# Loads of v on SyncE's queue instead of GpSimd's in the opening of a WKV recurrence kernel

## The chip, the cores and the metric

The kernel runs on one core of one Trainium2 chip. The metric is the device time of one execution in microseconds (us). A core has five engines with instruction streams of their own: TensorE (PE in the profile; PEld are its weight loads), VectorE (DVE), ScalarE (ACT), GpSimd (POOL) and SyncE (SP). Data moves between device memory and the core's SBUF by DMA, over 16 DMA engines that all queues of the core share. In this kernel two queues carry nearly everything: q0, whose transfers GpSimd issues in software, and q1, whose transfers SyncE issues.

## The reference

For each of 16 batches and each of 256 channels a recurrence runs over 2048 time steps, with a running maximum `pp` that keeps the exponentials in range:

```python
for t in range(seq_len):
    ww = u + kk
    qq = np.maximum(pp, ww)
    e1 = np.exp(pp - qq)
    e2 = np.exp(ww - qq)
    output[b, t, :] = (e1 * aa + e2 * vv) / (e1 * bb + e2 + 1e-08)
    ww = pp - w + kk
    qq = np.maximum(ww, kk)
    e1 = np.exp(ww - qq)
    e2 = np.exp(kk - qq)
    aa = e1 * aa + e2 * vv
    bb = e1 * bb + e2
    pp = qq
```

`k` and `v` are float32 of shape (16, 2048, 256), 33.55 MB each, and so is the output.

## The kernel before

The time steps are cut into 16 chunks of 128 steps, and each chunk into two halves of 64. A "pair" n is a tile of k and a tile of v with 128 time steps on the partitions, 4 batches and 256 channels: 512 KB each. There are 64 pairs; pair n belongs to chunk n // 4 and to the batches 4 * (n % 4) and the three after it. Below, kn and vn are the two tiles of pair n, counted from 0, so the fourth pair is n = 3.

For each pair these steps run; the short name in brackets is the one that the planner at the end of the kernel uses.

- Load k (`LK`, `load_k`) and v (`LV`, `load_v`).
- Bring k into the rounded 32-bit form that TensorE's fast float product reads, in a buffer of the pool `kr` (4 buffers). How this is done is chosen by `how(n)`: "D" rounds on VectorE and "P" on GpSimd (`RK`, `round_k`, line 200), both from a plain load into another buffer (`kf`, 5 buffers; for the first three pairs, a free output buffer `ot`). "C" loads with a conversion in the DMA, straight into `kr`, and needs no rounding. The string `FIRST` gives the choice for the first pairs, `PLAN` = "DDDP" repeats for the rest.
- Two products on TensorE, `rows` (`R`, line 207) and `logs` (`L`, line 213), form the logarithms of the weights in one of two PSUM tiles X, once with the matrix NLE (q = 0) and once with NLZ (q = 1). ScalarE takes the exponential of each (`X`, line 216).
- Cast v to bfloat16 (`CV`, `cast_v`, line 220): on VectorE for n < 10 (`EARLY`), on GpSimd from then on. Multiply it onto the weights on VectorE (`TV`, line 225), and sum each half chunk on TensorE (`S`, line 252).
- When a chunk's four pairs are summed, the state runs on: copy of the sums (`CS`, line 258), turn (`TU`, line 265), logarithm (`SL`, line 269), a scan and offsets on VectorE (lines 274 to 282), weights (`SW`, line 288), a scan (`CH`), a spread (`SS`) and the turn back (`TK`, line 309; `BK`, line 313).
- About ten pairs later the output follows: denominator and numerator on TensorE (`DEN`, `NUM`, line 329), logarithm and exponential of the denominator on ScalarE (lines 341 and 346), a product on VectorE (`MUL`, line 361) and three stores on SyncE (`ST`, lines 374 and 367). The first store is issued at 44.18 us.

Every step has a place, a number on one axis for all engines. The planner takes, again and again, the step with the lowest place whose predecessors are done and whose buffers are free, and writes its instructions into the streams of its engines; `keep_in_program_order` holds that order. On the chip each engine goes through its own stream in order and waits at an instruction until the semaphores that it needs are there. An issue of a load is such an instruction: if its buffer isn't free yet, all that is behind it on its engine waits too. The planner knows the buffers by the counts in `free`: 4 `kr` (K), 5 `kf` (KP), 4 `vr` for v (V), 8 `ot` (OT), 2 `vb` (VB). A `kr` buffer is free again after the second product `logs` of its pair; a `vr` buffer after the cast of its v.

In the opening, SyncE issues k0, k1, v0, k2, v1 and v2 (`BYSP` = 3) into output buffers. GpSimd then issues k3, k4, v3, k5, v4, k6, v5, k7, v6, k8, v7, k9, v8, k10, v9, k11, v10, k12, v11, k13, v12 in this order (lines 117, 121 and 114), rounds k11, casts v10, and goes on with loads and casts. k3 to k10 are "C". Matmuls on zeros into the tile TURN (line 155) are filled in between.

Of the kernel before, what the change touches and what calls it, by code (L numbers as in the profile page):

```python
# [15 lines left out]
def kernel(  # L16
# [9 lines left out]
    K = tc.keep_in_program_order  # L26
    PE, DVE, SC, POOL, SP = nc.tensor, nc.vector, nc.scalar, nc.gpsimd, nc.sync
# [11 lines left out]
    UNTIL = 16  # L39
    SHARE = 0.2  # L40
    BYSP = 3
    EARLY = 10
    PLAN = "DDDP"
    NK, NKP, NV, NVB, NRD, NOT = 4, 5, 4, 2, 2, 8
    RS = 2.0 ** -20
    CAP = 54.0
    BIG = 1e30
    FIRST = "DDDCCCCCCCC"
    VOT = 3
    XT = 8  # L50
    BYPOOL = 52
# [47 lines left out]
    def rows_of(x, n):  # L99
        c, p = divmod(n, 4)  # L100
        return x[4 * p:4 * p + 4, c * TC:(c + 1) * TC, :].rearrange("n t d -> t n d")
# [3 lines left out]
    def how(n):  # L105
        return "D" if n < BYSP else FIRST[n] if n < len(FIRST) else PLAN[n % len(PLAN)]

    def raw(pool, tag):
        return pool.tile([128, 4, Dm], F32, tag=tag, name=tag)

    def load_k(n):
        if how(n) != "C":
            KR[n] = raw(opool, "ot") if n < BYSP else raw(kppool, "kf")
            K((SP if n < BYSP else POOL).dma_start(out=KR[n], in_=rows_of(k, n)))  # L114
        else:
# [2 lines left out]

    def load_v(n):
        vr = raw(opool, "ot") if n < VOT else raw(vpool, "vr")  # L120
        K((SP if n < BYSP else POOL).dma_start(out=vr, in_=rows_of(v, n)))  # L121
        VR[n] = vr

    WUf = rpool.tile([128, 2, D], F32, tag="rd", name="WUf")[:, 0, 0:Dm]
# [93 lines left out]
    def cast_v(n):  # L218
        vb = vbpool.tile([128, 4, Dm], BF16, tag="vb", name="vb")
        K((DVE if n < EARLY else POOL).tensor_copy(vb, VR.pop(n)))  # L220
        VB[n] = vb
# [166 lines left out]
    for n in range(NP):  # L388
        c, j = divmod(n, 4)
        early = n < BYSP  # L390
        vb = "OT" if n < VOT else "V"
# [9 lines left out]
        else:  # L401
            free["OT"] -= 1
        step(("LV", n), n + P["LV"], load_v, (n,), [("LV", n - 1)] + ([("LK", n)] if n else []), vb)
        if how(n) != "C":
            step(("RK", n), put("RK"), round_k, (n,), [("LK", n), ("RK", n - 1)], "K", [kb])
# [91 lines left out]
```

## Time and profile before

| what | value | where it is from |
|---|---|---|
| median of 3 runs | 288.26 us (288.19 to 288.63) | times |
| profiled execution | 288.83 us, of which the span is 287.1 us | times, page |
| granted TensorE clock | 0.99 | page |
| PE, DVE, ACT, POOL busy | 268.5, 248.5, 259.0, 175.7 us | page, part 1 |
| moved by DMA | 101.20 MB, 352 GB/s mean | page, part 2 |
| q0 (GpSimd) | 65.42 MB in 21200 packets | page, part 3 |
| q1 (SyncE) | 35.14 MB in 37280 packets | page, part 3 |
| ACT busy, 17.2 to 44.6 us | 19.30 of 27.40 us | windows |
| ACT busy, 44.6 to 258 us | 209.50 of 213.40 us | windows |
| issue to landing of k3, k4, v3 | 8.9, 9.5, 10.3 us (issued 5.18, 6.08, 6.81) | DMA view, one window for each |
| issue to landing of k5, v4, k6, v5 | 6.6, 8.3, 8.8, 9.5 us (issued 12.00, 13.15, 14.21, 14.94) | DMA view, one window for each |
| q0's first tile data | after 9.8 us (until then 32 packets with less than 0.005 MB) | DMA view, 2 to 9.8 us |
| GpSimd before line 117 until PE has freed a buffer | 8.4 us in 6 waits, longest 4.3 | waits |
| GpSimd before line 121 until VectorE has cast a v | 7.0 us in 4 waits, longest 2.9 | waits |

The span is the time from the first to the last instruction on the core; the profiled execution's own time is 1.73 us longer. Landing is the moment at which the transfer's semaphore says that all of its bytes are there. In the timeline a row gives the start and the duration, the engine, the line, the operation, the output and input tiles and, in square brackets, how long the engine was idle just before and who ended that. The chain of waits is followed back from the last instruction to what released each step.

### The profile page before, as it was taken

The numbers are of one execution on the slowest core, as the hardware profiler recorded it, in microseconds if no ns is written. First come the engines' busy times: TensorE is split into PE (matmuls) and PEld (weight loads), VectorE is DVE, ScalarE is ACT, GpSimd is POOL, SyncE is SP. The second block draws the span as 40 slices with busy tenths as digits, with TensorE's granted clock in tenths as the row PEclk, the third lists the DMA queues.
The fourth block names the chain that finished last, engine by engine and source line by source line (L and its number), as shares of the span: only waits on it lengthen the run. The fifth ranks groups of instructions, "written<-read, shape, count | busy, mean of one in ns | idle before, by whom it ended". The sixth has DMA issues, their size and how long they took to land.

```text
span 287.1 us, 7961 instructions
## 1 busy us (share of the span) xinstructions
PE 268.5 (94%) x3215; PEld 134.8 (47%) x3215; DVE 248.5 (87%) x422; ACT 259.0 (90%) x291; POOL 175.7 (61%) x219
## 2 busy tenths in 40 slices
PE   6997999999999999999899999999999999997860
PEld 6443544454545455454445445454544454453530
DVE  5678799899898989897998989999898989889860
ACT  1786679999999999999999999999999999998990
POOL 8365476875757676874757686675766685421320
PEclk9999999999999999999999999999999999999996
DMA  6999999999999999999999999999999999955896
GB/s 220 349 351 346 349 350 352 393 382 390 381 392 389 391 392 389 389 353 388 391 393 387 381 391 388 390 376 394 383 391 369 393 391 382 369 160 142 217 275 191
DMA packets 58669, 101.20 MB, mean 352 GB/s; under 512 B 5152, under 2 KB 43688, under 8 KB 58632
## 3 DMA queue, kind: packets, MB, share of 16 engines
q0 software_dynamic: 21200, 65.42, 64.8%
q1 hardware_dynamic: 37280, 35.14, 36.5%
q8 instruction: 25, 0.41, 0.6%
q10 hardware_dynamic: 152, 0.14, 0.2%
q14 instruction: 12, 0.10, 0.1%
HBM read 67.12 MB, written 33.55 MB: 351 GB/s over the span
## 4 chain that ended last, share of the span: by engine, by line
PE 53%; DMA 23%; ACT 10%; DVE 8%; issue 3%; SPq 0%; POOL 0%; DVEq 0%; ACTq 0%; POOLq 0%
DMA out_dram<-ot 19%; PE X L213 14%; PE X L329 10%; PE num L329 8%; PE X L207 8%; PE TURN L155 7%; PE TOT L252 4%; ACT rd L341 4%; ACT EZR L216 3%; DVE ot L361 3%; DMA kr<-in_k_dram 3%; ACT rd L346 2%; DMA WUf<-in_u_dram 2%; DVE EZR L225 2%; PE TOT L265 1%
## 5 line engine op out<-in xcount | busy, mean ns | idle before, releaser
L216 ACT ACTIVATE EZR<-X 128x1024 bf16<-128x1024 f32 x128 | 126.8, 1014 | 11.5 <-PE X L213 11.5
L220 POOL CAST vb<-vr 128x1024 bf16<-128x1024 f32 x54 | 56.4, 1044 | 69.2 <-DVE EZR L225 67.8
L225 DVE TENSOR_TENSOR EZR<-EZR,vb 128x2048 bf16<-128x2048 bf16 x64 | 77.8, 1217 | 0.4
L361 DVE TENSOR_TENSOR ot<-num,rd 128x1024 f32<-128x1024 f32 x60 | 73.2, 1219 | 4.3 <-ACT rd L346 3.9
L346 ACT ACTIVATE rd<-rd 128x1024 f32<-128x1024 f32 (+1 forms) x65 | 68.0, 1046 | 2.0
L341 ACT ACTIVATE rd<-X 128x1024 f32<-128x1024 f32 (+1 forms) x65 | 65.8, 1012 | 2.9 <-PE X L329 1.1
L155 PE MATMUL TURN<-Z 128*128 128x192 bf16 x271 | 53.0, 262 | 1.5 <-DVE Z L139 1.4
L207 PE MATMUL X<-WU,CO 64*64 64x512 bf16 x512 | 51.9, 390 | 1.7 <-DVE WU L182 1.0
L121 POOL DMA_DIRECT2D vr<-in_v_dram x61 | 46.4, 761 | 7.0 <-DVE vb L220 7.0
L155 PEld LDWEIGHTS <-Z 128*128 128x128 bf16 x271 | 24.5, 101 | 50.6 <-issue 49.1
L213 PE MATMUL X<-kr,NLE 128*128 128x512 f32 x128 | 45.6, 437 | 0.7 <-DMA kr<-in_k_dram 0.7
L213 PE MATMUL X<-kr,NLZ 128*128 128x512 f32 x128 | 45.5, 436 | 0.0
L114 POOL DMA_DIRECT2D kf<-in_k_dram x53 | 40.2, 758 | 0.0
L200 DVE CAST kr<-kf 128x1024 fp32r<-128x1024 f32 x39 | 32.0, 849 | 4.2 <-DMA kf<-in_k_dram 4.0
L207 PEld LDWEIGHTS <-CO 64*64 64x64 bf16 x512 | 15.8, 104 | 32.2 <-issue 27.2
L329 PE MATMUL X<-EZR,S 64*64 64x512 bf16 x256 | 26.2, 394 | 1.7 <-ACT rd L341 1.0
L329 PE MATMUL num<-EZR,SN 64*64 64x512 bf16 x240 | 24.2, 386 | 2.2 <-DVE ot L361 2.2
L329 PE MATMUL X<-cb,Id 64*64 64x512 bf16 x256 | 25.8, 376 | 0.0
L329 PE MATMUL X<-EZR,Id 64*64 64x512 bf16 x256 | 25.8, 376 | 0.0
L252 PE MATMUL TOT<-EZR,OH 128*32 128x256 bf16 x512 | 23.7, 277 | 0.8 <-DVE EZR L225 0.5
L329 PE MATMUL num<-cb,IdN 64*64 64x512 bf16 x240 | 23.9, 376 | 0.0
L329 PE MATMUL num<-EZR,IdN 64*64 64x512 bf16 x240 | 23.9, 376 | 0.0
(69 smaller groups left out, 270.5 us busy)
## 6 DMA issues: line engine op xcount, KB each, us to landing
vr<-in_v_dram POOLq DMA_DIRECT2D x61, 512.0 KB, 7.9
kf<-in_k_dram POOLq DMA_DIRECT2D x53, 512.0 KB, 8.7
out_dram<-ot SPq DMA_DIRECT2D x64, 256.0 KB, 10.0
out_dram<-ot SPq DMA_DIRECT2D x116, 128.0 KB, 9.8
kr<-in_k_dram POOLq DMA_DIRECT2D x8, 512.0 KB, 9.5
ot<-in_k_dram SPq DMA_DIRECT2D x3, 512.0 KB, 5.2
ot<-in_v_dram SPq DMA_DIRECT2D x3, 512.0 KB, 8.4
out_dram<-ot POOLq DMA_DIRECT2D x11, 128.0 KB, 4.0
```

The lines of the kernel that those rows point to most:

```text
L114: K((SP if n < BYSP else POOL).dma_start(out=KR[n], in_=rows_of(k, n)))
L121: K((SP if n < BYSP else POOL).dma_start(out=vr, in_=rows_of(v, n)))
L155: K(PE.matmul(TURN[:, 0:192], Z[:, 0:128], Z, start=first, stop=True, skip_group_check=True))
L207: K(PE.matmul(X[a][o:o + HS, i, :].rearrange("p (n d) -> p n d", n=2), CO[r:r + HS, q, :], WU[r:r + HS, :].unsqueeze(1).broadcast_to([HS, ...
L213: K(PE.matmul(X[a][:, i, :], (NLE, NLZ)[q], km[:, i, :], start=False, stop=True, skip_group_check=True))
L216: K(SC.activation(ez(n)[:, q, 1], X[a], ACT.Exp))
L220: K((DVE if n < EARLY else POOL).tensor_copy(vb, VR.pop(n)))
L225: K(DVE.tensor_mul(ez(n)[:, :, 0], ez(n)[:, :, 1], vb.unsqueeze(1).broadcast_to([128, 2, 2, D])))
L329: K(PE.matmul(out_tile[o:o + HS, i, :], left, right, start=s == 0, stop=s == 2, tile_position=(r, o), skip_group_check=True))
L341: K(SC.activation(RD[n][:, i], X[a][:, i], ACT.Ln, scale=RS))
L346: K(SC.activation(RD[n][:, i], RD[n][:, i], ACT.Exp, scale=-1.0))
L361: K(DVE.tensor_mul(o.rearrange("p (i n) d -> p i (n d)", i=2)[:, i], NUM[n][:, i], RD[n][:, i]))
```

## The change

SyncE issues the loads of v for n = 3 to 13 too (`BYV` = 14; the destination buffers are the same as before), and k11 is loaded with its conversion ("C" as the twelfth letter of `FIRST`) instead of plain and then rounded on GpSimd. The step `RK 11` is gone, and k11 takes a `kr` buffer at its load. Nothing else is edited.

```diff
     BYSP = 3
+    BYV = 14
     EARLY = 10
...
-    FIRST = "DDDCCCCCCCC"
+    FIRST = "DDDCCCCCCCCC"
...
     def load_v(n):
         vr = raw(opool, "ot") if n < VOT else raw(vpool, "vr")
-        K((SP if n < BYSP else POOL).dma_start(out=vr, in_=rows_of(v, n)))
+        K((SP if n < BYV else POOL).dma_start(out=vr, in_=rows_of(v, n)))
```

In the changed program GpSimd's stream has k3 to k11, k12, k13, the cast of v10, k14, k15, the cast of v11, v14, k16, v15 and so on. SyncE's stream has its six loads as before, then v3 to v13, then the first store. The streams of TensorE, VectorE and ScalarE hold the same instructions in the same order as before.

## The prediction

> **What bounds the kernel now.** I read the page's forty slices first, to see when which unit is full.
>
> ```profile
> ACT  1786679999999999999999999999999999998990
> DMA  6999999999999999999999999999999999955896
> GB/s 220 349 351 346 349 350 352 393 382 390 381 392 389 391 392 389 389 353 388 391 393 387 381 391 388 390 376 394 383 391 369 393 391 382 369 160 142 217 275 191
> ```
>
> A slice is 7.18 us. From the seventh (43 us) to the end of the loads ACT is full; its work there is fixed, so the end moves by as much as the start of this full stretch moves. Before it ACT has gaps, and the DMA engines are full from the second slice on, at 346 to 352 GB/s of reads alone. All edits lie in this opening stretch, so I followed the chain of waits from 12 to 32 us, and the instructions at the two places where compute waits for a landing.
>
> ```profile
> 14.21 8.77 DMA kr<-in_k_dram
> 22.97 0.04 issue
> 23.02 0.72 PE X L213 x2
> ```
>
> ```profile
> 17.15 0.69 DVE L220 CAST vb<-vr 128x1024 bf16<-128x1024 f32 x1 [0.59 <-DMA vr<-in_v_dram]
> 23.02 0.72 PE L213 MATMUL X<-kr,NLE 128*128 128x512 f32 x2 [0.69 <-DMA kr<-in_k_dram]
> 25.43 0.28 ACT L269 ACTIVATE U<-TOT 128x128 f32<-128x128 f32 x1 [0.63 <-PE TOT L265]
> ```
>
> The chain runs through one load: k of the seventh pair (n=6; "kn" and "vn" below), issued at 14.21 and landed at 22.98, for which TensorE stood still 0.69 us. What follows hangs on it: the matmuls of n=6, then the turn of the sums (L265, 24.78), the logarithm on ACT (25.43), the state scan, the turn back (L309, 31.75), and from there TensorE has no gap over 0.11 us until after 45 us. So a later k6 moves the end one for one; an earlier one brings at most 0.69 us here. v3 (a wait of 0.59 us on VectorE) and v5 (0.17 us) are the only v that anything on VectorE waits for.
>
> Last, the queues: q0 holds what GpSimd issues, q1 what SyncE issues. Windows 10 to 13 us and 50 to 54 us:
>
> ```profile
> q1 hardware_dynamic: 514, 0.51, 62.7%
> q0 software_dynamic: 505, 0.51, 62.2%
> ...
> q0 software_dynamic: 344, 1.26, 80.5%
> q1 hardware_dynamic: 344, 0.32, 23.6%
> ```
>
> Columns: packets, MB, share of 16 engines. Where both queues have work they move the same number of packets. The first window has packets of 1 KB on both (k with conversion in q0, v in q1), so bytes are halved, 0.17 MB/us each. In the second q0's plain loads go in 4 KB packets and take four fifths. From 16 to 44 us q0 alone carries all data, 9.70 MB in 28 us, in the order of issue: k3 k4 v3 k5 v4 k6 v5 k7 v6 k8.
>
> **The change part by part.** The orders of TensorE, VectorE and ScalarE are the same in both programs. GpSimd loses eleven issues of v and one cast; SyncE gains the eleven behind its first six loads and ahead of its first store.
>
> *Issues taken from GpSimd:* 11 x 0.76 us (line L121) = 8.4 us, and the cast of k11 (L200, 1.04 us). Until 38 us GpSimd does nothing but issue loads and wait for buffers, so this time hides under its own waits (8.4 us in six waits for k's buffers); worth nothing on the path. k5 is issued at 12.00 and k6 at 14.21 because TensorE frees their buffers then; that stays.
>
> *k11* now goes straight into a `kr` buffer, freed by the second matmul of n=7 (28.2 us), so it can be issued at 28.5 at the earliest instead of 26.54. At q0's halved rate its bytes are through by some 37.8 us (nine tiles of 0.524 MB from 10.0, by the rate below) and land about 40, against 41.51 when TensorE reads it. Cost nothing; cover 1.5 us, more if TensorE is late.
>
> *v3 to v6* have free buffers and go out on SyncE at once, by about 9 us, instead of 6.81, 13.15, 14.94 and 17.14. At 10.0 q1 then still holds the rest of v1 and v2 (0.61 MB in the window from 10 us on) and four tiles more: 2.71 MB, 15.9 us of work at 0.17 MB/us, until 25.9; v7 is behind them by then, its buffer free once v3 is cast, some 18.5. So q1 never runs dry while k5 to k8 are on their way, and q0 gets half.
>
> *Price for k6.* Before, it was the sixth tile of q0: 6 x 0.524 = 3.15 MB, and q0 had moved 3.16 MB from 10.0 to 20.8; it landed 2.2 us after that (the slowest of the 16 engines and the completion). After, it is the fourth tile, 2.10 MB, but at 0.17 MB/us: 10.0 + 12.3 = 22.3, plus the same 2.2 is 24.5. That is 1.5 us later than 22.98. Bounds: k5 landed only 0.8 us behind its bytes, which would put k6 at 23.1, a loss of 0.1; and a wait of 0.69 that vanishes is a gain of 0.7. I take 1.5, since 2.2 is k6's own row.
>
> *The other landings.* v3 is third behind v1 and v2 in a halved queue: it starts at 13.6 instead of 14.5 and takes 3.1 us, landing at 17.7 instead of 17.1; the cast on VectorE goes 0.6 us later, the sums of n=2 on TensorE (18.99, just behind that product) too. k4 is through at 16.2, landed at 17.2, read at 17.33: no cost, cover 0.1. k5 is through at 19.2, landed between 20.0 and 21.4, read at 19.74 before: up to 1.7. Neither adds to the sum: with 1.7 TensorE reaches n=6 at 22.33 + 1.7 = 24.0, still ahead of 24.5. Behind it, k7 (25.4 + 2.2 = 27.6) is ready before 26.47 + 1.5 = 28.0, and k8 (28.5 + 2.2 = 30.7) is level with 29.08 + 1.5 = 30.6. v4 to v8 land within half a us of where they did.
>
> *Behind 38 us.* k12 and k13 are plain loads, and while they run q1's v10 and v11 get a fifth. v10 lands near 41 instead of 39.5; its cast on GpSimd (39.65) slips by about 1.3, and queued behind it are the issues of k14 and k15. v10's product runs on VectorE at 45.39 + 1.5, so 4 us of cover; k14, issued about 42, lands near 49 against 49.1 + 1.5. Nothing, but with 1.5 us of cover only. SyncE's first store (44.18) stands behind v13, whose buffer is free by 38.2.
>
> Sum: +1.5 us. On the profiled execution (span 287.1, time 288.83, so 1.73 around it) that is 288.6 and 290.3; it ran 0.57 us over the median, so against 288.26 I forecast **289.8 us**.
>
> **The rivals.** *Faster, k overtakes.* q0 now has only k in it, two tiles fewer ahead of k6. If it keeps more than half of the engines, k6 lands earlier. The point from which it decides: 1.59 MB (2.10 less 0.51) have to pass between 13.0 and 20.8, 0.20 MB/us, 58% of 0.35; at 0.22, 63%, the wait is gone and no more is won here, as TensorE comes at 22.33. Price -0.7: 287.6. For it: q1 alone ruled until 9.8 though q0 had been issued to at 5.18, so shares aren't always equal. Against: the 514 to 505 packets.
>
> *No change.* The bytes and the mean rate are the same, and if landings lag less than 2.2 us when two queues share, k6 comes at 23.1, a shift of 0.1: 288.4. For it: k3 to k5 lagged about 1.0 and less. Against: every q0 load from v4 on lagged 2.0 to 2.2. The Trainium skill speaks for this rival (DMA: Bandwidth & Descriptors, section "Issuing engines are not separate DMA queues"): DMAs of all issuing engines interleave on the same 16 DMA engines, and another issuer saves only the sequencer's time. By it the sum would be 0 here, as the saved 8.4 us lie under waits; the trace agrees on the total rate but shows that which queue a tile is in decides its share.
>
> *Slower still, q0 runs dry.* k3 was issued at 5.18 and q0 moved no tile data before 9.8, 4.7 us later. If k5 needs as much from its issue at 12.00, it starts at 16.7, when k4 is already through (16.2); k6 then is 0.5 later, and a late v10 holding k14 may add as much again: +2.0 to +2.7, 290.6.
>
> **How the numbers follow.** Less than 0.2% (0.58 us) can't be told from no change in this kernel. Forecast 0.48 (own range 289.0 to 290.3), slower still 0.14, no change 0.18, faster 0.20. So slower by over 0.2% is 0.62, within 0.18, faster 0.20. Half of the faster case is kept by reaching down to 287.6, its price, and of the slow one all but the worst by going to 290.8.
>
> **What would show it.** In the new profile the wait of L213 for kr at n=6 should be about 2 us in place of 0.69 and L309's first turn near 33.2 instead of 31.75; the window from 13 to 22 us should show equal packets in both queues. Wrong would be a wait for k under 0.7 us, more bytes in q0 than q1 there, or the delay present at 33 us and gone at 46.

## The result, and the profile after

| what | before | after |
|---|---|---|
| median of 9 runs | 288.26 us (288.13 to 289.29) | 289.93 us (289.20 to 291.91) |
| ratio of the times, with its 95% interval | | 1.0064 (1.0044 to 1.0083) |
| profiled execution, of which the span | 288.83, 287.1 us | 291.07, 289.2 us |

The change costs 1.7 us, or 0.64%, and the whole interval lies above the 0.2% that the prediction names as the least that can be told from no change. Where a ratio is given, runs over 1.5% above the fastest of the same kernel are left out, which touches only the experiment with v3 to v6, three of its twelve runs. The runs of the changed kernel also scatter more: 2.7 us between lowest and highest instead of 1.2. The profiled execution after is 1.1 us above its own median, the one before was 0.57 above its own, so the two traces differ by more (2.24 us) than the medians do (1.67 us).

The slices of the page after are these. A slice is 7.23 us.

```profile
ACT  1764678999999999999999999999999999998991
PEclk9997999999999999999999999999999999999997
DMA  7999999999999999999999999999999999974897
GB/s 223 344 342 348 350 348 324 379 314 391 387 387 364 365 390 374 397 383 390 390 386 376 356 391 384 395 383 394 390 393 387 386 392 347 375 220 136 242 268 205
```

The DMA engines are full in the opening as they were before, at 342 to 350 GB/s where it was 346 to 352. Between 13 and 22 us they moved 3.08 MB instead of 3.17, which at this rate is worth some 0.3 us. So the total rate is not where most of the time went. New is the fourth digit of PEclk: between 22 and 29 us TensorE was granted only about seven tenths of its clock.

The chain of waits of the kernel after, from 12 to 23 us (start, us, what), still goes through one load of k into a `kr` buffer. (The changed kernel has one line more near its top, so the L213 of before is L214 here, L220 is L221, and so on.)

```profile
12.24 9.93 DMA kr<-in_k_dram
22.17 0.04 issue
22.22 0.73 PE X L214 x2
```

This load is k5, not k6. The timeline of TensorE on that line shows what it did to the products of the sixth to eighth pair (n = 5, 6, 7; a row of NLE and a row of NLZ for each):

```profile
22.22 0.73 PE L214 MATMUL X<-kr,NLE 128*128 128x512 f32 x2 [2.14 <-DMA kr<-in_k_dram]
23.26 1.20 PE L214 MATMUL X<-kr,NLZ 128*128 128x512 f32 x2
25.55 1.20 PE L214 MATMUL X<-kr,NLE 128*128 128x512 f32 x2
27.07 0.71 PE L214 MATMUL X<-kr,NLZ 128*128 128x512 f32 x2
29.49 0.71 PE L214 MATMUL X<-kr,NLE 128*128 128x512 f32 x2
```

TensorE stood still 2.14 us for k5. Before, the same row had come without a wait:

```profile
19.74 0.71 PE L213 MATMUL X<-kr,NLE 128*128 128x512 f32 x2
```

The wait of 0.69 us for k6 is gone from its row at 25.55: k6 landed at 25.07, while TensorE was still busy. And two rows that take 0.71 us elsewhere took 1.20. The windows (start:end, length, then busy time and instructions of each engine, the granted clock of TensorE, DMA share, GB/s) say why; first the one of before, then those of after:

```profile
20.00:22.20 2.20, 2.20 (x22) 0.78 (x21) 0.46 (x3) 1.84 (x3) 1.29 (x3) 1.00 1.36 348
```

```profile
core 0: us, PE busy (x) PEld busy (x) DVE busy (x) ACT busy (x) POOL busy (x), PEclk, DMA share, GB/s
20.00:22.20 2.20, 0.08 (x1) 0.00 (x0) 0.15 (x1) 0.28 (x1) 0.26 (x1) 1.00 1.26 336
22.20:24.00 1.80, 1.78 (x9) 0.93 (x9) 0.00 (x0) 1.01 (x1) 0.00 (x0) 0.80 1.23 337
24.00:26.00 2.00, 2.00 (x16) 0.77 (x15) 0.94 (x2) 1.03 (x2) 0.74 (x1) 0.50 1.26 340
26.00:28.00 2.00, 2.00 (x13) 0.85 (x13) 1.90 (x3) 1.02 (x1) 0.00 (x0) 0.83 1.29 348
28.00:30.00 2.00, 1.63 (x19) 0.88 (x18) 1.16 (x7) 1.19 (x2) 0.74 (x1) 1.00 1.53 375
```

From 20 to 22.2 us, where it was busy throughout before, TensorE is now idle, VectorE, ScalarE and GpSimd are nearly idle too, and the DMA engines are full: all engines wait for one tile. In windows of 0.2 us the granted clock is at 0.50 from 23.3 to 26.7 us and at 1.00 on both sides.

The difference between the two traces at the same instruction adds up like this. Until k5 there is 0.1 to 0.2 (k4 was read at 17.48 instead of 17.33). The first product of n = 5 is late by 2.48 us (22.22 against 19.74), that of n = 6 by 2.53 (25.55 against 23.02). At full clock TensorE would have been through with n = 5 some 2.59 us after its start, as before (19.74 to 22.33), so at 24.81, and would have waited for k6 until 25.11, 2.09 us later than before; the slow clock made it 0.44 later still. The second of n = 6 is late by 3.02 (27.07 against 24.05), 0.49 more of slow clock. Later 0.36 is taken up again, and the turn back of the state's sums is late by 2.66 us, in the timelines of before and after:

```profile
31.75 0.39 PE L309 MATMUL TURN<-Id,CB 128*128 128x128 bf16 x4
```

```profile
34.41 0.39 PE L310 MATMUL TURN<-Id,CB 128*128 128x128 bf16 x4
```

ScalarE enters its full stretch (44.6 us before) 2.67 us late. At the last product of the output the difference is 3.09 us (283.49 against 280.40), of which the last stores give back 1.0: that leaves the 2.1 us between the spans.

How the two queues shared the engines is seen in the view of the DMA queues (packets, MB, share of 16 engines). The window that the prediction named, 13 to 22 us, has before:

```profile
q0 software_dynamic: 1990, 3.06, 135.9%
q1 hardware_dynamic: 109, 0.10, 4.1%
```

and after:

```profile
q1 hardware_dynamic: 1673, 1.65, 65.7%
q0 software_dynamic: 1426, 1.41, 57.9%
```

So q0 moved less than half of what it had. The two numbers of packets are not quite equal, and two shorter windows of the kernel after, 11 to 16 and 16.2 to 17.4 us, show where they part:

```profile
q1 hardware_dynamic: 848, 0.85, 62.6%
q0 software_dynamic: 846, 0.85, 62.4%
...
q1 hardware_dynamic: 347, 0.35, 88.0%
q0 software_dynamic: 107, 0.09, 29.2%
```

First they take turns packet by packet, at 0.17 MB/us each. Before, q0 had to share only until v2 was through, at some 13 us, and then had the engines alone; now k4 goes on at half a rate (landed 17.08 instead of 15.56). Then q0 runs nearly dry, because k4's bytes are through and those of k5, issued at 12.24, are only beginning to come some 5 us after their issue. This stretch holds 240 of the 247 packets by which the queues differ from 13 to 22 us. From about 17.3 on k5 has half a rate again. By the same view q0 has moved the 1.57 MB of k3, k4 and k5 at 20.2 us and the 2.10 MB up to the end of k6 at 23.35; the two landed at 22.17 and 25.07, 2.0 and 1.7 us after their bytes. The tile that gained is v4: it landed at 19.17, ahead of k5, where before it had come behind k5 (18.58) at 21.44, though its cast comes later than the product that reads k5.

### The profile page after: what moved, and what is told of

Same layout as the page of the kernel before. It is cut to its first block, busy times and chain, and to the rows that moved or that the text cites. A ratio compares the mean times of both kernels' runs of the same rounds, so it can differ in the third digit from the quotient of the medians.

```text
span 289.2 us, 7967 instructions
## 1 busy us (share of the span) xinstructions
PE 270.4 (93%) x3215; PEld 135.2 (47%) x3215; DVE 248.8 (86%) x422; ACT 259.5 (90%) x291; POOL 166.7 (58%) x207
## 4 chain that ended last, share of the span: by engine, by line
PE 39%; DMA 35%; DVE 10%; ACT 9%; issue 5%; POOL 1%; SPq 0%; DVEq 0%; POOLq 0%; ACTq 0%
DMA out_dram<-ot 26%; PE X L214 10%; PE X L330 7%; PE num L330 6%; PE X L208 5%; PE TURN L156 5%; DVE ot L362 4%; ACT rd L342 4%; DMA kf<-in_k_dram 3%; PE TOT L253 3%; DMA kr<-in_k_dram 3%; ACT rd L347 3%; ACT EZR L217 2%; DVE EZR L226 2%; DMA WUf<-in_u_dram 2%
## 5 line engine op out<-in xcount | busy, mean ns | idle before, releaser
L221 POOL CAST vb<-vr 128x1024 bf16<-128x1024 f32 x54 | 56.9, 1053 | 78.4 <-DVE EZR L226 77.8
L156 PE MATMUL TURN<-Z 128*128 128x192 bf16 x271 | 53.7, 266 | 1.5 <-DVE Z L140 1.4
L156 PEld LDWEIGHTS <-Z 128*128 128x128 bf16 x271 | 25.1, 103 | 50.9 <-issue 49.3
L214 PE MATMUL X<-kr,NLE 128*128 128x512 f32 x128 | 46.0, 441 | 2.1 <-DMA kr<-in_k_dram 2.1
L214 PE MATMUL X<-kr,NLZ 128*128 128x512 f32 x128 | 45.9, 441 | 0.0
L122 POOL DMA_DIRECT2D vr<-in_v_dram x50 | 37.8, 756 | 0.0
L201 DVE CAST kr<-kf 128x1024 fp32r<-128x1024 f32 x39 | 33.5, 888 | 4.6 <-DMA kf<-in_k_dram 4.6
```

The source lines that it names most:

```text
L122: K((SP if n < BYV else POOL).dma_start(out=vr, in_=rows_of(v, n)))
L156: K(PE.matmul(TURN[:, 0:192], Z[:, 0:128], Z, start=first, stop=True, skip_group_check=True))
L214: K(PE.matmul(X[a][:, i, :], (NLE, NLZ)[q], km[:, i, :], start=False, stop=True, skip_group_check=True))
```

## The experiments

They were timed in three groups, with the kernel before run beside each group (medians 288.40, 288.46 and 288.31 us). The ratio is to that. "Shift of the opening" is by how much the products of n = 8 or the turn back come later in the profile than in the first profile of before. The experiments keep the line numbers of before.

### Which of the two edits: v alone, k11 alone

Only the queue of v3 to v13:

```diff
-        K((SP if n < BYSP else POOL).dma_start(out=vr, in_=rows_of(v, n)))
+        K((SP if n < 14 else POOL).dma_start(out=vr, in_=rows_of(v, n)))
```

> SyncE issues v3 to v13, and k11 stays a plain load rounded by GpSimd. Theory (v3 to v6 in the other queue halve the share of k5 and k6; TensorE waits some 2 us for k5 and then runs some 4 us at a granted clock near 0.5 to 0.8): the whole loss is here, ratio 1.005 to 1.008, a wait of L213 for kr of about 2 us near 20 to 22 us. Rival (the new place of k11 costs, as it needs a kr buffer and leaves later): ratio near 1.000.

Measured: 290.52 us, ratio 1.0083 (1.0051 to 1.0116), opening shifted by 2.62 us. The timeline has the row of the whole change, with nearly the same wait, and here this row itself is slow (1.22 us):

```profile
22.17 1.22 PE L213 MATMUL X<-kr,NLE 128*128 128x512 f32 x2 [1.99 <-DMA kr<-in_k_dram]
```

Only the load of k11:

```diff
-    FIRST = "DDDCCCCCCCC"
+    FIRST = "DDDCCCCCCCCC"
```

> Only k11 is loaded with its conversion; all v from the fourth on stay on GpSimd. Theory: nothing on the path, ratio 1.000 within 0.002, the wait for k6 stays near 0.7 us. Rival (k11 costs): ratio 1.005 or more.

Measured: 288.62 us, ratio 1.0003 (0.9985 to 1.0020). k6 landed at 22.87 and was read at 22.91. So the move of v is the whole loss, and k11 is worth nothing.

### Which of the v: v3 to v6, v7 to v13, v3

Both have the `FIRST` of the change; the conditions for SyncE are

```diff
-        K((SP if n < BYSP else POOL).dma_start(out=vr, in_=rows_of(v, n)))
+        K((SP if n < 7 else POOL).dma_start(out=vr, in_=rows_of(v, n)))
...
+        K((SP if n < BYSP or 6 < n < 14 else POOL).dma_start(out=vr, in_=rows_of(v, n)))
```

> SyncE issues v3 to v6 only; v7 to v13 go back to GpSimd; k11 as in the change. Theory: these four tiles are what stands beside k4 to k6, so the loss stays, ratio 1.004 to 1.008, with the wait for k5 of 1.5 to 2.5 us. Rival (the loss arises later, from v10 to v13 beside 4 KB packets and ahead of the first stores): ratio under 1.002.

Measured: 289.72 us, ratio 1.0051 (1.0021 to 1.0080). Both are from nine of its runs. The wait is there (2.08 us ahead of n = 5 at 22.14), and so is the slow clock, for 6.8 us in the profiled execution, which at 292.29 us is above the median and whose opening is shifted by 3.9. This part is enough for the loss of the whole.

> The other half: v3 to v6 on GpSimd, v7 to v13 on SyncE. Theory: k5 and k6 come as in the kernel before, ratio 1.000 to 1.003 (k8 to k10 may share their bytes with v7 to v9, with little behind it). Rival (the loss arises later): ratio 1.005 or more, and no long wait for kr before 25 us.

Measured: 293.53 us, ratio 1.0164 (1.0128 to 1.0199), a clear miss: the later v alone cost more than the whole change. k5 was not late (n = 5 at 20.25), and n = 6 waited 0.18 us. The wait sits further on, ahead of n = 8, after one of 0.81 ahead of n = 7:

```profile
32.19 0.72 PE L213 MATMUL X<-kr,NLE 128*128 128x512 f32 x2 [2.23 <-DMA kr<-in_k_dram]
```

It is the same mechanism at another tile. With v3 to v6 back in q0, k8 is the tenth tile there and was issued at 19.91, and now v7 and those behind it take turns with it in q1: k8 landed at 32.15 instead of 28.97, and v7, which is needed later, at 27.23 instead of 30.48. In the whole change k8 is the sixth tile of q0 and landed at 30.32. What fell is my claim that only k5 and k6 can lose; the early v on SyncE shield k8 from the late ones. The opening is shifted by 3.1 us (the turn back at 34.87), so the landings account for about 3.1 of the 5.1 us between the medians; the profiled execution, 291.77 us, is itself 1.8 us under its median. Where the rest arises is not shown; four of the other five runs have a lower mean clock than it.

> Of the v that move only v3 goes to SyncE; k11 as in the change. Theory (each tile of v on SyncE's queue pushes back the tiles of k that it runs beside): one tile is worth at most its 1.5 us, and k5 and k6 have v4 and v5 behind or ahead of them in q0 as before; k5 lands by 19.8 and k6 within 1 us of 22.97: ratio 1.000 to 1.003. Rival (any v on SyncE makes q0 run dry and costs the whole 2 us): ratio 1.005 or more.

This is the whole change with `n < 4` as the condition. Measured: 288.27 us, ratio 1.0002 (0.9979 to 1.0024); k5 landed at 18.56, and the row of n = 6 is that of before:

```profile
23.12 0.74 PE L213 MATMUL X<-kr,NLE 128*128 128x512 f32 x2 [0.78 <-DMA kr<-in_k_dram]
```

With one v moved q0 stays ahead: in the window from 16.2 to 17.4 us it moved 371 packets and q1 106. Here too q0 ran nearly dry, from 16.0 to 16.4 us (28 packets against 132 of q1), since k5's bytes began only 4.4 us after its issue at 12.04. But q1 was through with v3 soon after, and then q0 had the engines alone. So the sharing after 16.8 us needs v4 and those behind it in q1, and a short dry stretch without it cost nothing that shows.

### Packets: k plain instead of converted

If queues take turns by packets, k loaded plainly, in 4 KB packets, should get four fifths of the bytes. This is the first experiment with all k up to k11 plain and rounded by GpSimd, which adds eight casts to the one of k11:

```diff
-    FIRST = "DDDCCCCCCCC"
+    FIRST = "DDDPPPPPPPPP"
```

> The changed kernel with k3 to k11 as plain loads (packets of 4 KB instead of 1 KB, issued up to two tiles earlier) and rounded by GpSimd. Theory (the queues take turns by packets, so the bytes of a queue go by its packet size): q0 now gets four fifths, k5 is there in time and no product waits for it, but v2 comes some 2.5 us later (landing about 17.2 instead of 14.6) and VectorE waits for it at the cast of v2, for about 2 us; ratio 1.005 to 1.012. Rival (what counts is that software-issued loads start late or run slower beside the other queue): L213 waits for k5 as in the change and v2 lands by 15.

Measured: 295.66 us, ratio 1.0266 (1.0230 to 1.0303): the direction was right, the size too small. In the window from 11 to 15 us:

```profile
q0 software_dynamic: 301, 1.10, 80.4%
q1 hardware_dynamic: 299, 0.31, 25.2%
```

The number of packets is equal again and the bytes are as 3.5 to 1, so turns go by packets. No product waited for k any more. Now v2 was late (landed 17.55; before, 14.58), and VectorE waited for it:

```profile
17.64 1.65 DVE L220 CAST vb<-ot 128x1024 bf16<-128x1024 f32 x1 [2.93 <-DMA ot<-in_v_dram]
19.21 2.04 DVE L225 TENSOR_TENSOR EZR<-EZR,vb 128x2048 bf16<-128x2048 bf16 x1
```

GpSimd, with roundings among its issues, issued k6 only at 16.54 (14.21 before). The opening was shifted by 8.5 us, more than the 7.2 us of the medians.

### The slow clock: zeros into the gap

The change was run once more, and beside it the change with 20 products on zeros ahead of n = 5, so that TensorE is not idle while it waits for k5.

```diff
-    ZAT = {"DEN 0": 4, "TU 1": 4, "R 0 11": 4}
+    ZAT = {"DEN 0": 4, "TU 1": 4, "R 0 11": 4, "L 0 5": 20}
```

> The changed kernel once more, beside the next three on the same chip. Ratio 1.005 to 1.008, the wait for k5 about 2.1 us.

> The changed kernel with 20 matmuls on zeros (some 2 us) in TensorE's stream before the first product of n=5, so that TensorE works while it would wait for k5. Theory (the wait itself costs some 1.5 us against the kernel before, and the idle time drops TensorE's granted clock, which costs the rest and makes the times scatter): the clock stays at 1.00 from 22 to 28 us, the runs lie closer together than those of the change, and the median is 0.5 to 1.2 us under it. Rival (the clock drop costs nothing, only the landing counts): same as the change within 0.3 us, or slower if the zeros reach past the landing.

Measured: the change 290.07 us (288.73 to 292.92), ratio 1.0052 (1.0026 to 1.0079); with zeros 290.00 us (289.04 to 290.76), ratio 1.0053 (1.0034 to 1.0073). The zeros did what they were for; in the profile the clock stays at full through the wait and after it:

```profile
20.00:22.20 2.20, 2.20 (x26) 1.71 (x23) 0.18 (x1) 0.06 (x1) 0.04 (x1) 1.00 1.25 337
22.20:24.00 1.80, 1.80 (x21) 0.71 (x20) 0.37 (x2) 1.74 (x2) 0.46 (x1) 1.00 1.25 340
```

There k5 was read at 21.50, n = 6 waited 0.36 us for k6 at 24.47, and the opening was shifted by 1.6 us, by landings alone. The longest run came down by 2.2 us, but the median did not move, where 0.5 to 1.2 us were expected. That fits a slow clock that occurs in the long runs alone, but the kernel before, run beside these, also spreads over 2.4 us (287.25 to 289.67 in 29 runs), so it is not shown, nor is the share of the clock in the median. Of the twelve runs of the change, the six with a mean granted clock of 0.992 or more took 288.73 to 290.25 us, the six below 290.01 to 292.92.

### Is it the second queue, or the order?

In the kernel before, all v stay on GpSimd, but v4 and v5 are issued ahead of k5, whose bytes then come behind theirs in one queue:

```diff
-           "SN 0": 8.15, "FR 1": 8.95, "CV 9": 8.0, "SW 1": 9.6, "RK 11": 9.1}
+           "SN 0": 8.15, "FR 1": 8.95, "CV 9": 8.0, "SW 1": 9.6, "RK 11": 9.1, "LV 4": 0.5, "LV 5": 0.51}
...
-        step(("LV", n), n + P["LV"], load_v, (n,), [("LV", n - 1)] + ([("LK", n)] if n else []), vb)
+        step(("LV", n), n + P["LV"], load_v, (n,), [("LV", n - 1)] + ([("LK", n)] if n not in (0, 4, 5) else []), vb)
```

> The kernel before, with all v from the fourth on GpSimd's queue, but v4 and v5 issued ahead of k5 (order k3 k4 v3 v4 v5 k5 k6 k7 v6 ...). Theory (what costs is the order in which the bytes come; the second queue only changes that order): k5 is now the sixth tile of its queue, its bytes through at 20.8 and landed between 21.6 and 23.0 instead of 18.58, so L213 waits for k5 some 2 to 3 us and the ratio is 1.005 to 1.012, with no load on SyncE. Rival (the loss belongs to two queues running side by side, each at half rate): one queue alone keeps its full rate, ratio under 1.003.

Measured: 292.20 us, ratio 1.0138 (1.0107 to 1.0168). The timeline, and the queues from 15 to 22 us:

```profile
22.87 1.22 PE L213 MATMUL X<-kr,NLE 128*128 128x512 f32 x2 [1.81 <-DMA kr<-in_k_dram]
```

```profile
q0 software_dynamic: 1360, 2.40, 131.4%
q8 instruction: 1, 0.02, 1.0%
q1 hardware_dynamic: 4, 0.00, 0.2%
```

k5 landed at 22.83, 0.7 us later than in the change, and the opening was shifted by 3.3 us, with q0 alone at work at 2.40 MB in 7 us. Nothing shares the engines there and no queue is dry. That v bytes go ahead of k5's is enough for the loss, through whichever queue.

### Can k6's wait be had?

In the kernel before, the place of v4 alone is set so that k6 is issued ahead of it:

```diff
-           "SN 0": 8.15, "FR 1": 8.95, "CV 9": 8.0, "SW 1": 9.6, "RK 11": 9.1}
+           "SN 0": 8.15, "FR 1": 8.95, "CV 9": 8.0, "SW 1": 9.6, "RK 11": 9.1, "LV 4": 1.56}
```

> The kernel before with k6 issued ahead of v4 on GpSimd's queue. Theory: k6 comes a tile (1.5 us) earlier, its wait of 0.69 us is gone, and v4 lands up to 1.5 us later than 21.44, when VectorE's cast of v4 (22.20) waits 0.3 to 0.8 us for it; the state scan (25.74) then hangs on the casts of v4 and v5: gain 0 to 0.5 us, ratio 0.998 to 1.000. Rival (v4 and v5 carry as much weight as k6): the scan is no earlier than before, ratio 1.000 to 1.002.

Measured: 288.45 us, ratio 1.0009 (0.9989 to 1.0029). k6 landed at 21.32 and n = 6 started at 22.37 with no wait, 0.65 us earlier than before. Then a wait for v4 (0.43 us on VectorE) and one for k8 took its place:

```profile
28.96 0.74 PE L213 MATMUL X<-kr,NLE 128*128 128x512 f32 x2 [0.25 <-DMA kr<-in_k_dram]
```

At n = 8 the opening is 0.1 us early. An earlier k6 is worth nothing, since the bytes that it overtakes are needed next. No order that was tried beats the kernel before.

## Why the prediction was right, point by point

*The mechanism* was right. With v in q1 the two queues take turns packet by packet, k comes at half rate, TensorE waits about 2 us for a tile of k, and the delay stays until the end. The forecast of 289.8 us stands against 289.93. The v move alone gives the loss; k11 alone and one v alone give none. "Carried one for one" held: the shift is 2.66 us at 34 us and 2.67 at 44.6. It then grows by some 0.4 that I can't assign, and the end of the stores gives 1.0 back.

*The step that failed* is the landing of k5. The prediction had it "landed between 20.0 and 21.4" and concluded "Neither adds to the sum". It landed at 22.17, and the long wait is there; the place named in "what would show it", a wait of about 2 us at n = 6, shows none. The term that was mis-sized is the time at which q0's bytes are through: 20.2 instead of 19.2 for k5, for two reasons. q0's first data came about 0.4 us later than before (15 packets of q0 from 10.0 to 10.4 us instead of 63; k3 was issued at 5.64 instead of 5.18), so that it had moved 0.46 MB by 13 us instead of 0.51. And q0 ran nearly dry between k4 and k5, 0.09 MB from 16.2 to 17.4 us where half the rate is some 0.2, which is worth about 0.7 us. That is the premise of the "slower still" rival, and the forecast "q0 gets half" left it out. Why a load takes 4 to 5 us from its issue to its first data no run shows. From the bytes to the landing it then took 2.0 us, inside the 0.8 to 2.2 that were allowed. k6's bytes were through 1.05 us late too (23.35 for 22.3) and it landed at 25.07 instead of 24.5, since 2.2 was 0.5 too much for it. By landings alone k6 still ended last, as the sum had it, with TensorE at hand only 0.3 us before it.

*The clock after the wait* was not in the sum at all. In the profiled execution it cost about 0.9 us at n = 6 (0.44 and 0.49), of which 0.36 was taken up later. With the clock kept full (zeros) the opening is shifted by 1.6 us, close to the +1.5 of the forecast: there k5 landed at 21.46 and the product of n = 6 waited for k6 until 24.47. In the change itself landings and clock together made 2.7. The median has part of that 2.7, with a share of the clock that isn't known, so the agreement to 0.1 us is in part luck. Nor is the run with zeros the change less the clock alone: its k3 was issued at 5.18 as before and its k5 at 11.89, so its tiles land earlier for that reason too. How often the clock drops in runs without a profile can't be seen; the spread of their mean clocks suggests that it does in some and not in others.

*"q1 never runs dry"* held for k5 and k6 (340 packets of each queue from 22 to 24 us) and not for k8. VectorE's casts of v4 and v5 came late with everything else, so v8 was issued only at 26.11 (23.30 before) and v9 at 28.04 (25.79), and v8's bytes began only about 29.7 us, some 3.6 us after its issue. So the slow start is not peculiar to q0. From 28 to 30 us q0 moved 701 packets and q1 61. That is why k8 landed at 30.32 without costing anything. How close that is, the experiment with v7 to v13 alone shows.

*The v behind v3* did not keep to "within half a us of where they did": v4 landed 2.3 us earlier, v6 at 26.31 instead of 27.46 and v7 at 29.46 instead of 30.48. That is the other side of k's loss.

*What was costed at nothing* stayed there: GpSimd's saved time became longer waits (for `kr` buffers in the first 46 us, 19.2 us after, 8.4 before), k4 landed at 17.08 and was read at 17.48, v3 landed at 16.88 (17.06 before, not the 17.7 forecast, so the cast was not late). Past 38 us v10's cast was at 40.25 instead of 39.65, held by VectorE and not by its load, and k14 was issued at 41.64, near the 42 forecast; no instruction of TensorE waited for a load there.

*The rivals.* "Faster" needed q0 to keep more than half; it got half or less, and an earlier k6 gains nothing anyway. For "no change", the Trainium skill (DMA: Bandwidth & Descriptors, section "Issuing engines are not separate DMA queues") says that DMAs of all issuers interleave on the same engines. That is what the packet counts show, and the reordered kernel with all v on GpSimd confirms that a second queue is not needed for the loss. But the rule concerns bandwidth. It is silent on which tile lands first, and that was worth most of the 0.64%.

## What to carry to other kernels

Where the DMA engines are full, issuing a load from another engine buys no bandwidth; it changes the order in which tiles land. In this kernel queues with work took turns packet by packet, so whatever moves to a second queue early goes beside, and partly ahead of, the tiles that compute needs next. Look for the load that ends last at the head of the critical chain, and count the bytes that will pass before its last one, in all queues together, before and after; the issue time that GpSimd saved here was worth nothing, as it only waited longer for buffers.

## What the runs showed of the hardware that was not expected

TensorE's granted clock fell to 0.50 after idle gaps of only about 2 us: 1.81 (v4 and v5 first), 1.99 (v alone), 2.08 and 2.14 us (the change, twice), 2.08 (v3 to v6). It stayed there for 3.41 us in the change, in v alone and in v4 and v5 first, and for twice as long, 6.83 us, in v3 to v6 and in k plain. After a gap of 2.23 us, in the profile of v7 to v13, it stayed at 1.00, though four of the other five runs of that kernel have a lower mean clock (0.980 to 0.987 against 0.989) and took 1.65 to 2.5 us longer. So the drop comes after some gaps and not after others, and that can widen the scatter of the kernel.

Where it comes can be worked out from the traces. The clock changes only at points that lie whole steps of 3.41 us apart: down at 23.28 and up at 26.69 us in the change, 22.17 and 25.58 in v alone, 21.93 and 28.75 in v3 to v6. In the step that ends where the clock falls, TensorE was idle for 1.80 (v4 and v5 first), 1.86 (v3 to v6), 1.99 (v alone), 2.08 and 2.14 us (the change), in each case over half of the step. In the profile of v7 to v13 a boundary counted back from a later fall of the clock, at 283.83 us, lies at 31.25, inside the gap from 29.96 to 32.19. That leaves 1.3 us of idle time to one step and 0.9 to the next, and the clock stayed. In v3 to v6 and k plain the first slow step still held 0.2 and 0.5 us of idle time and a second slow one followed; where it held none the clock came back. This was read out of the traces afterwards, and no run was made to test it.

The Trainium skill (TensorE: Matmul & The Clock Gate, section "What's actually happening") has the clock at half after at least one idle window of about 3.4 us, and the window runs freely. The length and the free running agree with the steps of 3.41 us. That a window must be idle as a whole does not: 1.80 us in one were enough, and here the measurement decides.

VectorE's cast took 1.65 instead of 0.69 us and its product 2.04 instead of 1.22 while GpSimd was rounding and issuing in the same stretch (k plain). That one caused the other was not tried by itself.
